# Three distances in a hand-ordered TensorE stream: mLSTM's last transposes, the softmax weights' transposes, and the last inputs of the output projections

## The chip, the cores and the metric

The kernel runs on one core of one Trainium2 chip. The metric is the device time of one execution in microseconds (us). The kernel before was run three times: 1007.92, 1008.61 and 1011.15 us, a median of 1008.61. Engines are named as in the profile: PE is TensorE (its matmuls and transposes), PEld its weight loads, DVE is VectorE, ACT is ScalarE, POOL is GpSimd, SP issues most DMAs.

## The reference

A token sequence of 256 positions with 1024 features goes through two blocks in float32. The first block has two layers. The even layer projects x to a short gated convolution (1024 wide) and to eight heads of a gated delta rule, and projects the 2048 outputs back; the odd layer does the same with 16 heads of HGRN2 (2048 outputs). Behind each come a layer norm on the residual sum and a gated addition. The second block is an attention mixer and a gated feed-forward part of width 2816. The mixer matters most here:

```python
y_fox  = _fox_attention(...)    # 6 heads, causal softmax with forget-gate bias
h_ml   = _mlstm(...)            # 4 heads
y_ml   = _from_heads(_rms(h_ml)) * ml_h_g * sigmoid(mo)
y_moba = _moba_attention(...)   # 6 heads, softmax with ALiBi bias (256 tokens: one block)
return jnp.concatenate([y_fox, y_ml, y_moba], axis=-1)
...
x = x + g1 * (y @ w_out)
```

## The kernel before, in words

Activations lie with features on partitions, in tiles of 128 features by 256 tokens. Every float32 operand of a large product is split into a high part (`hi`, `xh`, `yh`, a rounding by ACT) and a low part (`lo`, `xl`, `yl`, a subtraction by DVE), and a product of a 128 x 128 weight block is three matmuls: high by high, high weight by low input, low weight by high input. All weights of all layers lie in one stream of chunks of 16 blocks; `Stream.take` hands them out in the order in which the products use them, and splits half a chunk (8 blocks) two chunks ahead. A half can be split when the buffers of an older half are free, that is when PE has done that half's products.

PE is the only engine whose order is written by hand; the compiler's scheduler orders the others from the program's dependencies. The main line of the program issues the dense products. Beside it run generators, the side work of heads: recurrences, softmax, norms, transposes. `Side` keeps a virtual clock that advances by 0.65 with every two products (every three matmuls on 512 columns in `dense_tok`). A generator that says `yield 4.95` is taken up again when the virtual clock is 4.95 further, and its PE instructions are put into PE's stream at that place. So the number in a `yield` is a distance: how much dense work stands in PE's stream between one step of a head and the next. If the inputs of the next step aren't ready when PE comes to it, PE waits, as it works in order.

The stages follow each other as `even`, `odd`, `mixer`, `ffn`. In the mixer, `lstm` computes the four mLSTM heads in scores (`sms`), then values, divides, normalizes (DVE, with a power step on POOL, tiles `lo_`), and after its last distance transposes both token halves back (`pt`), multiplies by the gate (`y`), and splits into `yh`, `yl` as inputs 3 and 4 of the output projection. `heads` computes three groups of four query/key blocks with `dense_tok`; `head_norm` normalizes and transposes them (`sq`) into `kq` by ACT and DVE copies. `softmax_pair` does two heads: bias (transposes of `cs` and DVE), scores from `kq`, maximum, exponential and normalization into `pr`; after the distance, PE transposes the six 128 x 128 pieces of `pr` (two PSUM buffers a pair, 12 transposes for the two pairs of a group), ACT copies them (`pts`), and PE multiplies with the values. All small PSUM results of side work share four buffers (`psm`), taken in turn; a step waits until the buffer of four allocations earlier has been read. Dense results have four others (`psd`).

`out_plan` gives the order of an output projection: the first inputs over all eight output blocks, then the last `tail` = 4 inputs bank by bank (a PSUM bank holds two output blocks), so that banks finish one after the other. When a bank is finished, DVE updates x (`ready`), PE transposes x (`ln_stats`, `rms_stats`), and DVE or ACT takes the statistics. The same lists order the weight stream.

Around the change, in the program as it was:

```python
n = len(ks) - tail
return [(k, m) for k in ks[:n] for m in range(8)] + \
    [(k, m) for j in range(4) for k in ks[n:] for m in (2 * j, 2 * j + 1)]
...
OUT_PLANS = [out_plan([0, 1, 2, 3, 4, 5, 6, 8, 9, 10, 11, 7, 12, 13, 14, 15], 4),
             out_plan(list(range(16)), 4), out_plan([3, 4, 0, 1, 2, 5, 6, 7], 4)]
```

Of the kernel before, what the change touches and what calls it, by code (L numbers as in the profile page):

```python
# [60 lines left out]
def out_plan(ks, tail):  # L61


    n = len(ks) - tail
    return [(k, m) for k in ks[:n] for m in range(8)] + \
        [(k, m) for j in range(4) for k in ks[n:] for m in (2 * j, 2 * j + 1)]

# [2 lines left out]
QK_BLOCKS = [0, 1, 6, 7, 2, 3, 8, 9, 4, 5, 10, 11]  # L72

OUT_PLANS = [out_plan([0, 1, 2, 3, 4, 5, 6, 8, 9, 10, 11, 7, 12, 13, 14, 15], 4),
             out_plan(list(range(16)), 4), out_plan([3, 4, 0, 1, 2, 5, 6, 7], 4)]
DOWN_GROUPS = [[0, 1], [2, 3], [4, 5], [6], [7]]

# [122 lines left out]
class Net:  # L200
# [1020 lines left out]
    def softmax_pair(self, p_, kq, vs, yh, yl):  # L1221

        nc, ep = self.nc, self.ep
        t2 = lambda shape, tag, bufs=2: ep.tile(shape, F32, tag=tag, bufs=bufs, name=self.nm(tag))
        yield from self.wait(lambda: {(p_ // 2, 0), (p_ // 2, 1)} <= self.kqdone)
        pts = []
        for e in range(2):
            h = 2 * p_ + e
            rows = slice(64 * e, 64 * e + 64)
            q, k = kq[rows, p_], kq[rows, 6 + p_]  # L1230
            bias = t2([P, 3 * P], "bias", 3)
            if p_ < 3:
                t = self.ps("m")
                for a_ in range(2):
                    self.tr(t[:, a_ * P:(a_ + 1) * P], self.cs[:, a_, h:h + 1].to_broadcast([P, P]))
                self.tt(bias[:, :P], t[:, :P], self.c("cneg"), ALU.add)
                nc.scalar.copy(bias[:, P:2 * P], t[:, :P])
                self.tt(bias[:, 2 * P:], t[:, P:T], self.c("cneg"), ALU.add)
            else:
                nc.gpsimd.tensor_scalar(bias, self.dist, float(2.0 ** (-8.0 * (h - 5) / 6)), None, ALU.mult)  # L1240
            s = self.ps("m")
            self.mm(s[:, :P], q[:, :P], k[:, :P])
            self.mm(s[:, P:3 * P], q[:, P:], k)
            pr = t2([P, 3 * P], "pr", 6)
            mx, nm, sm = t2([P, 2], "smx"), t2([P, 2], "snm"), t2([P, 2], "ssm")
            for a_, c in ((0, slice(0, P)), (1, slice(P, 3 * P))):
                nc.vector.tensor_tensor_reduce(pr[:, c], s[:, c], bias[:, c], 1.0, -3e38, ALU.add, ALU.max, mx[:, a_:a_ + 1])
                self.ts(nm[:, a_:a_ + 1], mx[:, a_:a_ + 1], -1.0)
                self.act(pr[:, c], pr[:, c], AF.Exp, bias=nm[:, a_:a_ + 1], accum_out=sm[:, a_:a_ + 1])
            nc.vector.reciprocal(sm, sm)  # L1250
            for a_, c in ((0, slice(0, P)), (1, slice(P, 3 * P))):
                self.ts(pr[:, c], pr[:, c], sm[:, a_:a_ + 1])
            pts.append(pr)
            if e == 0:
                yield 0.65
        yield 4.95
        pt2 = []
        for e in range(2):

            pt = self.ps("m")  # L1260
            pn = t2([P, 3 * P], "pts", 6)
            for b in range(3):
                self.tr(pt[:, b * P:(b + 1) * P], pts[e][:, b * P:(b + 1) * P])
            nc.scalar.copy(pn, pt[:, :3 * P])
            pt2.append(pn)
        yield 0.65
        yield from self.wait(lambda: p_ // 2 in self.vdone or 1 in self.vdone)
        py = self.ps("m")
        for e in range(2):
            h = 2 * p_ + e  # L1270
            rows = slice(64 * e, 64 * e + 64)
            vc = 256 + 64 * h
            self.mm(py[rows, :T], vs[:, 0, vc:vc + 64], pt2[e][:, :T], stop=False)
            self.mm(py[rows, P:T], vs[:, 1, vc:vc + 64], pt2[e][:, T:], start=False)
        y = t2([P, T], "y2", 2)
        nc.scalar.copy(y, py[:, :T])
        n = p_ if p_ < 3 else p_ + 2
        self.split(yh[:, n], yl[:, n], y)
        self.ydone.add(n)
# [32 lines left out]
    def lstm(self, vs, yh, yl):  # L1312
        nc, ep = self.nc, self.ep
        t2 = lambda shape, tag, bufs=2: ep.tile(shape, F32, tag=tag, bufs=bufs, name=self.nm(tag))
        yield from self.wait(lambda: self.gated)
        va = ep.tile([P, 2, 4, 65], F32, name="va")
        nc.gpsimd.memset(va[:, :, :, 64:], 1.0)
        nc.gpsimd.tensor_copy(va[:, :, :, :64], vs[:, :, :256].rearrange("p a (h d) -> p a h d", d=64))
        sms = []
        for h in range(4):  # L1320
            rows = slice(64 * (h % 2), 64 * (h % 2) + 64)
            q, k = self.mqk[rows, h // 2], self.mqk[rows, 2 + h // 2]
            e = self.ps("m")
            for a_ in range(2):
                c = slice(2 * a_ * P, (2 * a_ + 1) * P)
                self.tr(e[:, c], self.mx[:, a_, h:h + 1].to_broadcast([P, P]))
                self.mm(e[:, c], self.bf["id"], self.bf["pos"], start=False)
            self.tr(e[:, P:2 * P], self.mx[:, 1, h:h + 1].to_broadcast([P, P]))
            et, sm = t2([P, 3 * P], "et"), t2([P, 3 * P], "smt", 4)
            self.act(et[:, :T], e[:, :T], AF.Exp, scale=-1.0, bias=self.r[:, 0, h:h + 1])  # L1330
            self.act(et[:, T:], e[:, T:3 * P], AF.Exp, scale=-1.0, bias=self.r[:, 1, h:h + 1])
            s = self.ps("m")
            self.mm(s[:, :T], k[:, :P], q)
            self.mm(s[:, T:3 * P], k[:, P:], q[:, P:])
            self.stt(sm, s[:, :3 * P], 1.0 / 32, et)
            sms.append(sm)
            yield 0.65
        os = []
        for a_ in range(2):
            pn = self.ps("m")  # L1340
            for h in range(4):
                c = slice(65 * h, 65 * h + 65)
                if a_ == 0:
                    self.mm(pn[:, c], sms[h][:, :P], va[:, 0, h])
                else:
                    self.mm(pn[:, c], sms[h][:, P:T], va[:, 0, h], stop=False)
                    self.mm(pn[:, c], sms[h][:, T:], va[:, 1, h], start=False)
            v = pn[:, :260].rearrange("p (h d) -> p h d", d=65)
            dn, ss, rs = t2([P, 4], "ldn"), t2([P, 4], "lss"), t2([P, 4], "lrs")
            self.ts(dn, v[:, :, 64], -1.0)  # L1350
            self.tt(dn, dn, v[:, :, 64], ALU.max)
            self.tt(dn, dn, self.em[:, a_], ALU.max)
            nc.vector.reciprocal(dn, dn)
            o, sq = t2([P, 4, 64], "lo_"), t2([P, 4, 64], "lsq")
            self.tt(o, v[:, :, :64], dn.unsqueeze(2).to_broadcast([P, 4, 64]))
            self.act(sq, o, AF.Square)
            nc.vector.tensor_reduce(ss, sq, AX.X, ALU.add)
            self.ts(ss, ss, 1.0 / 64, 1e-6)
            self.rsqrt(rs, ss)
            self.tt(o, o, rs.unsqueeze(2).to_broadcast([P, 4, 64]))  # L1360
            os.append(o)
            yield 0.65
        yield 4.0
        pt = self.ps("m")
        for a_ in range(2):
            for j in range(2):
                self.tr(pt[:, (2 * j + a_) * P:(2 * j + a_ + 1) * P], os[a_][:, 2 * j:2 * j + 2].rearrange("p h d -> p (h d)"))
        for j in range(2):
            y = t2([P, T], "y2", 2)
            self.stt(y, pt[:, j * T:(j + 1) * T], self.prm["ml_h_g"][:, j:j + 1], self.mo[:, j])  # L1370
            self.split(yh[:, 3 + j], yl[:, 3 + j], y)
            self.ydone.add(3 + j)
# [126 lines left out]
```

## Time and profile before

| | us |
|---|---|
| median of three runs | 1008.61 |
| the profiled execution, its time | 1007.96 |
| its span, from first to last instruction | 1006.1 |
| PE busy | 978.8 |
| DVE busy | 759.1 |
| ACT busy | 554.2 |
| POOL busy | 49.9 |

The profile is of one execution. A busy PE is not PE at its peak: the ends of matmuls are modelled and overlap with the next one's start, so the pitch of a stream is read from its starts. "Idle before" is the gap to the end of the instruction before on the same engine, and the arrow names what ended it. The granted clock is TensorE's, as a share of 2.4 GHz.

### The profile page before, as it was taken

Reading aid. Unit: us, or ns where it says so; the run is one execution under the profiler, and the core shown is the slowest. Engines: PE = TensorE matmul, PEld = TensorE weight load, DVE = VectorE, ACT = ScalarE, POOL = GpSimd, SP = SyncE. Lnnn points to the kernel's source line nnn. Section 1 sums busy time; section 2 is a strip of 40 time slices with the busy share of each in tenths; the row PEclk is TensorE's granted clock in tenths of the full one; section 3 lists DMA queues with packets and bytes.
Section 4 is the critical chain, followed back from the end, with each engine's and each line's share of the span. In section 5 each row is a group of like instructions: output and inputs, shape, how many; then the busy total and the mean of one; then the engine's idle time right before and its main releaser. Section 6 shows DMA issues by size and latency. Waiting matters only on the chain. (4 is left out here: it accounts for less than half of the span.)

```text
span 1006.1 us, 19098 instructions
## 1 busy us (share of the span) xinstructions
PE 978.8 (97%) x7622; PEld 935.6 (93%) x7622; DVE 759.1 (75%) x1459; ACT 554.2 (55%) x1098; POOL 49.9 (5%) x59
## 2 busy tenths in 40 slices
PE   6999999999999999999999999999999999999998
PEld 5999999999999999998989999997777999999998
DVE  5888876888667979889797986889577597665542
ACT  6765556644553864554545534677456674444430
POOL 1000000000000000000000000000223000000000
PEclk9999999999999999999999999999989999999999
DMA  7545523445553595655556563364323547654540
GB/s 283 191 147 177 169 86 126 166 164 177 200 195 126 185 374 208 222 201 201 210 192 230 185 215 132 111 231 135 116 84 126 189 148 272 221 199 168 185 172 22
DMA packets 34617, 179.52 MB, mean 178 GB/s; under 512 B 7648, under 2 KB 8672, under 8 KB 16608
## 3 DMA queue, kind: packets, MB, share of 16 engines
q1 hardware_dynamic: 34096, 177.71, 49.8%
q8 instruction: 60, 0.98, 0.4%
q10 hardware_dynamic: 432, 0.59, 0.2%
q14 instruction: 29, 0.24, 0.1%
HBM read 176.97 MB, written 1.31 MB: 177 GB/s over the span
## 5 line engine op out<-in xcount | busy, mean ns | idle before, releaser
L226 DVE TENSOR_TENSOR lo<-raw,hi 128x1024 fp32r<-128x1024 f32 x280 | 340.6, 1221 | 122.5 <-ACT hi L226 121.8
L226 ACT CAST hi<-raw 128x1024 fp32r<-128x1024 f32 x280 | 292.0, 1047 | 228.3 <-PE psd L312 217.6
L312 PE MATMUL psd<-xh,hi 128*128 128x256 f32 (+1 forms) x1296 | 375.6, 290 | 0.5 <-ACT hi L226 0.5
L312 PE MATMUL psd<-xl,hi 128*128 128x256 f32 (+1 forms) x1296 | 366.7, 283 | 0.4 <-DVE xl L331 0.4
L312 PE MATMUL psd<-xh,lo 128*128 128x256 f32 (+1 forms) x1296 | 366.2, 283 | 0.8 <-DVE lo L226 0.8
L312 PEld LDWEIGHTS psd<-xl,hi 128*128 128x128 f32 x1296 | 245.5, 189 | 1.4 <-DVE xl L331 1.0
L312 PEld LDWEIGHTS psd<-xh,hi 128*128 128x128 f32 x1296 | 245.0, 189 | 1.8 <-ACT hi L226 0.8
L312 PEld LDWEIGHTS psd<-xh,lo 128*128 128x128 f32 x1296 | 245.5, 189 | 1.0 <-DVE lo L226 1.0
L312 PE MATMUL psd<-yh,hi 128*128 128x256 f32 x448 | 130.6, 291 | 0.4 <-ACT yh L334 0.2
L312 PE MATMUL psd<-yl,hi 128*128 128x256 f32 x448 | 126.3, 282 | 1.2 <-DVE yl L235 1.0
L312 PE MATMUL psd<-yh,lo 128*128 128x256 f32 x448 | 126.6, 283 | 0.0
L312 PEld LDWEIGHTS psd<-yl,hi 128*128 128x128 f32 x448 | 84.8, 189 | 1.8 <-DVE yl L235 1.2
L312 PEld LDWEIGHTS psd<-yh,hi 128*128 128x128 f32 x448 | 84.7, 189 | 1.9 <-issue 0.8
L312 PEld LDWEIGHTS psd<-yh,lo 128*128 128x128 f32 x448 | 83.9, 187 | 0.0
L312 PE MATMUL psd<-hi,xh 128*128 128x512 f32 x144 | 60.9, 423 | 0.5 <-DVE lsrc L322 0.5
L1011 DVE SCALAR_TENSOR_TENSOR wa<-wa,cr 128x1024 f32<-128x1024 f32 x48 | 58.4, 1218 | 3.3 <-DMA wa<-in_w_ada_dram 2.7
L312 PE MATMUL psd<-hi,xl 128*128 128x512 f32 x144 | 57.9, 402 | 0.0
L312 PE MATMUL psd<-lo,xh 128*128 128x512 f32 x144 | 57.6, 400 | 0.0
L312 PE MATMUL psd<-al,hi 128*128 128x256 f32 x176 | 49.8, 283 | 0.0
L312 PE MATMUL psd<-ah,lo 128*128 128x256 f32 x176 | 49.7, 283 | 0.0
L312 PE MATMUL psd<-ah,hi 128*128 128x256 f32 x176 | 49.3, 280 | 0.0
L334 ACT ACTIVATE kp<-k 128x512 f32<-128x512 f32 x28 | 19.0, 679 | 33.0 <-DVE k L322 26.2
(338 smaller groups left out, 1397.8 us busy)
## 6 DMA issues: line engine op xcount, KB each, us to landing
raw<-in_w_dram SPq DMA_DIRECT2D x140, 1024.0 KB, 4.8
wa<-in_w_ada_dram SPq DMA_DIRECT2D x48, 512.0 KB, 4.5
cr<-in_c_dram SPq DMA_DIRECT2D x3, 512.0 KB, 5.7
out_dram<-fo SPq DMA_DIRECT2D x3, 256.0 KB, 2.1
cst<-in_cst_dram SPq DMA_DIRECT2D x1, 580.0 KB, 8.3
x<-in_xT_dram ACTq DMA_DIRECT2D x2, 256.0 KB, 4.0
x<-in_xT_dram SPq DMA_DIRECT2D x2, 256.0 KB, 4.8
lev<-in_lev_dram SPq DMA_DIRECT2D x1, 508.0 KB, 4.0
```

The costliest lines, as they stand in the source:

```text
L226: for i in self.nc.scalar.copy(hi, r), self.nc.vector.tensor_tensor(lo, r, hi.bitcast(F32), ALU.subtract):
L312: self.nc.tensor.matmul(out, lhsT, rhs, start=start, stop=stop, skip_group_check=True, **k)
L334: return self.nc.scalar.activation(out, a, f, bias=bias, scale=scale, **k)
L1011: self.tc.keep_in_program_order(nc.vector.scalar_tensor_tensor(w, w, 1.0, c, ALU.mult, ALU.mult, accum_out=self.md(j)[:, i % 8:i % 8 + 1]))
```

## The change

Three edits. `out_plan`: for the first two banks, the last two inputs are now used after the two before them have been used in both banks; banks 2 and 3 keep their order. The function serves all three output projections, and the weights in memory follow it. `softmax_pair`: the distance before the transposes of `pr` goes from 4.95 to 5.85. `lstm`: the distance before the last transposes goes from 4.0 to 9.75.

```diff
     n = len(ks) - tail
-    return [(k, m) for k in ks[:n] for m in range(8)] + \
-        [(k, m) for j in range(4) for k in ks[n:] for m in (2 * j, 2 * j + 1)]
+    bank = lambda ks, j: [(k, m) for k in ks for m in (2 * j, 2 * j + 1)]
+    return [(k, m) for k in ks[:n] for m in range(8)] + bank(ks[n:-2], 0) + bank(ks[n:-2], 1) + \
+        bank(ks[-2:], 0) + bank(ks[-2:], 1) + bank(ks[n:], 2) + bank(ks[n:], 3)
...
-        yield 4.95
+        yield 5.85
         pt2 = []
...
-        yield 4.0
+        yield 9.75
         pt = self.ps("m")
```

On PE, the program before has mLSTM's last transposes (`lo_`, into `psm_8684`) among the products of the second group of query and key blocks (`psd_8599`, `psd_8600`):

```order
4836 L312 MATMUL psd_8599<-hi_8480,xh_7704 128x512
4837 L312 MATMUL psd_8599<-hi_8480,xl_7705 128x512
4838 L312 MATMUL psd_8599<-lo_8481,xh_7704 128x512
4839 L315 MATMUL psm_8684<-cst,lo__1398_8591 128x128 x2
4840 L315 MATMUL psm_8684<-cst,lo__1409_8626 128x128 x2
4841 L312 MATMUL psd_8600<-hi_8480,xh_7704 128x512
```

The changed program has products there, and the transposes stand behind the last scores (`kq`) of the first softmax group:

```order
4874 L317 MATMUL psm_8808<-cst,ag_cs 128x128 x2
4875 L314 MATMUL psm_8814<-kq_8423 128x128
4876 L314 MATMUL psm_8814<-kq_8423 128x256
4877 L314 MATMUL psd_8774<-hi_8603,xh_7704 128x512
4878 L314 MATMUL psd_8774<-hi_8603,xl_7705 128x512
4879 L314 MATMUL psd_8774<-lo_8604,xh_7704 128x512
4880 L317 MATMUL psm_8849<-cst,lo__1398_8591 128x128 x2
4881 L317 MATMUL psm_8849<-cst,lo__1409_8626 128x128 x2
4882 L314 MATMUL psd_8773<-hi_8603,xh_7704 128x512
```

They moved past 18 products, eight transposes of `sq` and all scores of the group; 27 products follow before the transposes of `pr` (24 stood there in all before, now 30 from the last scores on).

On DVE, the end of the first softmax group in the program before: `sq` and `hss` are the next group's head norm, `lo` the weights' low parts, `pr` the normalizations, the second pair of which is the last:

```order
1054 L1199 TENSOR_REDUCE hss_8852<-sq_8851 128x8
1055 L1250 RECIPROCAL ssm_8810<-ssm_8810 128x2
1056 L226 TENSOR_TENSOR lo_8869<-raw_8788,hi_8868 128x1024
1057 L326 TENSOR_SCALAR pr_8807<-pr_8807,ssm_8810 128x128
1058 L326 TENSOR_SCALAR pr_8807<-pr_8807,ssm_8810 128x256
1059 L1250 RECIPROCAL ssm_8833<-ssm_8833 128x2
1060 L328 TENSOR_SCALAR hss_8852<-hss_8852 128x8
1061 L226 TENSOR_TENSOR lo_8887<-raw_8884,hi_8886 128x1024
1062 L326 TENSOR_SCALAR pr_8830<-pr_8830,ssm_8833 128x128
1063 L326 TENSOR_SCALAR pr_8830<-pr_8830,ssm_8833 128x256
1064 L322 TENSOR_TENSOR sq_8851<-psd_8600,hrs_8853 128x512
```

The same place in the changed program, where `y` and `yl` are mLSTM's outputs:

```order
1052 L328 TENSOR_SCALAR pr_8794<-pr_8794,ssm_8797 128x128
1053 L328 TENSOR_SCALAR pr_8794<-pr_8794,ssm_8797 128x256
1054 L330 TENSOR_SCALAR hss_8839<-hss_8839 128x8
1055 L333 SCALAR_TENSOR_TENSOR y_1466_8854<-psm_8849,prm,yl_1289_8005 128x256
1056 L1252 RECIPROCAL ssm_8820<-ssm_8820 128x2
1057 L324 TENSOR_TENSOR sq_8838<-psd_8600,hrs_8840 128x512
1058 L328 TENSOR_SCALAR pr_8817<-pr_8817,ssm_8820 128x128
1059 L328 TENSOR_SCALAR pr_8817<-pr_8817,ssm_8820 128x256
1060 L237 TENSOR_TENSOR yl_1287_8003<-y_1466_8854,yh_1286_8002 128x256
1061 L333 SCALAR_TENSOR_TENSOR y_1467_8858<-psm_8849,prm,yl_1289_8005 128x256
1062 L228 TENSOR_TENSOR lo_8869<-raw_8775,hi_8868 128x1024
```

The two weight subtractions moved behind the last `pr`, and the next group's `sq`, which needs POOL's `hrs`, moved ahead of it. `psm_8849` is the buffer that the fourth set of `pr` transposes takes next (`psm_8917`).

On DVE, the odd layer's output projection in the program before, where `x` is the update of a finished bank (`psd_6954` is bank 0) and BN_STATS the statistics:

```order
847 L226 TENSOR_TENSOR lo_7474<-raw_7442,hi_7473 128x1024
848 L331 SCALAR_TENSOR_TENSOR x_80<-x_80,psd_6954 128x512
849 L226 TENSOR_TENSOR lo_7512<-raw_7509,hi_7511 128x1024
850 L792 BN_STATS st_6953<-psm_7489 128x6 x2
851 L331 SCALAR_TENSOR_TENSOR x_80<-x_80,psd_6955 128x512
```

And in the changed program:

```order
847 L228 TENSOR_TENSOR lo_7473<-raw_7442,hi_7472 128x1024
848 L228 TENSOR_TENSOR lo_7512<-raw_7509,hi_7511 128x1024
849 L333 SCALAR_TENSOR_TENSOR x_80<-x_80,psd_6954 128x512
850 L333 SCALAR_TENSOR_TENSOR x_80<-x_80,psd_6955 128x512
851 L794 BN_STATS st_6953<-psm_7502 128x6 x2
```

A weight subtraction moved ahead of the update of bank 0. On PE the transposes of x for bank 0 moved 12 products (of 256 columns) later, those of the other banks not at all.

## Rows read from the trace of the kernel before

**Rows 1.** The page: span, and busy time of PE

```profile
span 1006.1 us, 19098 instructions
PE 978.8 (97%) x7622; PEld 935.6 (93%) x7622; DVE 759.1 (75%) x1459; ACT 554.2 (55%) x1098; POOL 49.9 (5%) x59
```

**Rows 2.** Waits of PE: who for whom, us in total, times, longest

```profile
PE psm L315 <- DVE lo__1398_8591 L322: 1.8, 1, 1.8
...
PE psm L315 <- DVE lo__1409_8626 L322: 1.6, 1, 1.6
...
PE psm L315 <- DVE pr L326: 1.3, 2, 1.1
PE psd L312 <- DVE yl L235: 1.0, 1, 1.0
```

**Rows 3.** Stretches around mLSTM's transposes: busy time by engine, granted clock

```profile
core 0: us, PE busy (x) PEld busy (x) DVE busy (x) ACT busy (x) POOL busy (x), PEclk, DMA share, GB/s
...
726.40:730.80 4.40, 0.97 (x6) 0.55 (x5) 2.35 (x6) 0.78 (x1) 2.46 (x2) 0.79 0.02 4
730.80:737.30 6.50, 6.50 (x20) 5.08 (x19) 3.56 (x6) 1.84 (x3) 0.00 (x0) 0.62 0.47 161
737.30:744.40 7.10, 7.10 (x39) 4.77 (x37) 4.70 (x27) 5.59 (x19) 1.64 (x1) 1.00 0.00 0
```

**Rows 4.** Timeline of PE around mLSTM's transposes: start us, us, what, idle before

```profile
726.23 0.39 PE L312 MATMUL psd<-lo,xh 128*128 128x512 f32 x1
728.47 0.41 PE L315 MATMUL psm<-cst,lo__1398_8591 128*128 128x128 f32 x2 [1.85 <-DVE lo__1398_8591 L322]
730.45 0.69 PE L315 MATMUL psm<-cst,lo__1409_8626 128*128 128x128 f32 x2 [1.58 <-DVE lo__1409_8626 L322]
730.79 0.77 PE L312 MATMUL psd<-hi,xh 128*128 128x512 f32 x1
...
737.31 1.03 PE L315 MATMUL psm<-cst,sq 128*128 128x128 f32 x8
...
739.19 0.97 PE L312 MATMUL psm<-kq 64*128 64x128 f32 x4
```

**Rows 5.** Timeline of PE: first product after the scores, first transposes of pr

```profile
744.47 0.50 PE L312 MATMUL psd<-hi,xh 128*128 128x512 f32 x1
...
750.19 1.14 PE L315 MATMUL psm<-cst,pr 128*128 128x128 f32 x9
```

**Rows 6.** Timeline of DVE: weight subtraction, copies to kq, last bias read

```profile
730.31 1.22 DVE L226 TENSOR_TENSOR lo<-raw,hi 128x1024 fp32r<-128x1024 f32 x1
...
738.60 0.29 DVE L1213 COPY kq<-psm 128x128 f32<-128x128 f32 x1 [1.71 <-ACT kq L334]
...
739.12 0.29 DVE L1213 COPY kq<-psm 128x128 f32<-128x128 f32 x1
...
745.33 0.27 DVE L322 TENSOR_TENSOR bias<-psm,cst 128x128 f32<-128x128 f32 x1
```

**Rows 7.** Timeline of POOL: the power steps of two head norms

```profile
741.13 1.64 POOL L339 TENSOR_TENSOR hrs<-hss,mhalf 128x8 f32<-128x8 f32 x1 [11.20 <-DVE hss L328]
750.32 2.48 POOL L339 TENSOR_TENSOR hrs<-hss,mhalf 128x8 f32<-128x8 f32 x1 [7.55 <-DVE hss L328]
```

**Rows 8.** Timeline of PE and DVE in the even layer's output projection

```profile
301.99 0.38 PE L312 MATMUL psd<-yh,hi 128*128 128x256 f32 x1 [0.16 <-ACT yh L234]
...
303.41 0.39 PE L312 MATMUL psd<-yl,hi 128*128 128x256 f32 x1 [1.04 <-DVE yl L235]
...
302.94 0.42 DVE L235 TENSOR_TENSOR yl<-y,yh 128x256 fp32r<-128x256 f32 x1
```

**Rows 9.** Timeline of DVE and PE in the odd layer's output projection

```profile
621.82 0.69 DVE L331 SCALAR_TENSOR_TENSOR x<-x,psd 128x512 f32<-128x512 f32 x1 [0.69 <-PE psd L312]
622.79 1.23 DVE L226 TENSOR_TENSOR lo<-raw,hi 128x1024 fp32r<-128x1024 f32 x1 [0.27 <-ACT hi L226]
...
622.94 0.28 PE L312 MATMUL psd<-yh,lo 128*128 128x256 f32 x1
623.06 0.60 PE L315 MATMUL psm<-cst,x 128*128 128x128 f32 x4
623.41 0.37 PE L312 MATMUL psd<-yh,hi 128*128 128x256 f32 x1
```

## The prediction

> **What bounds the kernel now.** I read the page's busy shares first. TensorE (PE) is busy for 978.8 of 1006.1 us [rows 1]; the reader should see that no other engine can set the end unless PE stops for it, and that all of PE's idle time together is 27.3 us. So an edit that moves PE's instructions is worth what PE waits at the places it moves, plus what TensorE's clock loses there. Second view: what PE waited for. The largest waits after the start are the two for mLSTM's tiles `lo_` (1.8 and 1.6 us); the softmax weights `pr` cost 1.3 us in two waits, and one wait of 1.0 us is for `yl`, an input of an output projection [rows 2]. These are the three things that the change moves. Third view: the stretches around the `lo_` waits. The granted clock is 0.79 in the stretch of the waits and 0.62 in the 6.5 us behind it, in which PE is always busy [rows 3]: between these waits TensorE falls from 2.4 to 1.2 GHz, and the busy stretch behind them pays for it.
>
> **mLSTM's transposes.** In the timeline [rows 4] the last product before them starts at 726.23. A product on 512 columns takes 0.238 us from start to start: 24 of them fill 744.47 to 750.19 [rows 5]. So PE is free at 726.47, but the first two transposes start at 728.47, the others at 730.45, and the next product at 730.79: 4.32 us, of which four transposes need 0.35 (what four of x take further on, 623.06 to 623.41). The 18 products behind them take 730.79 to 737.31, 6.52 us where 18 x 0.238 = 4.28 would do: 2.24 us lost to the clock. Without the transposes PE would start those 18 at 726.47, end them at 730.75, and reach the first score product (`kq`) 1.88 us later (737.31 to 739.19 in before [rows 4]), at 732.63 instead of 739.19. That is 6.56 us.
>
> What is late next: the score products need four VectorE (DVE) copies to `kq`. DVE's own chain is not moved by PE's freedom. It finishes the second `lo_` at 730.4 as before, because that waits for GpSimd, and then two weight subtractions stand ahead of the copies in the order of after: 730.31 + 2 x 1.2 = 732.7 [rows 6]. The third copy starts 0.52 later (738.60 to 739.12) and takes 0.29: 733.5. The second score product needs it. In before it was ready at 739.41, so the stage moves up by 5.9 us, not 6.56.
>
> The transposes themselves (0.35) now stand three products behind the last score product. They take the PSUM buffer that the bias transposes of four allocations earlier used, and DVE reads that last at 745.33 + 0.27 = 745.60 [rows 6], in after at 739.70. PE arrives at 744.47 - 5.9 + 3 x 0.238 = 739.28. I take a new wait of 0.4. Not seen in before, it lies between 0 (if DVE is that much earlier) and 0.9 (one more weight subtraction of 1.2 ahead of it, less the 0.3 that the copy takes). Sum for this edit: 5.9 - 0.35 - 0.4 = 5.15.
>
> Queued behind the moved steps: on DVE, `y` of head pair one stands just ahead of the last softmax normalization, and `y` of pair two behind it. The second `y` also frees the PSUM buffer that the fourth set of softmax transposes takes, so PE waits there for DVE, and DVE before that for GpSimd's power step (`hrs`). GpSimd started that step at 750.32 in before [rows 7], behind a weight subtraction of 1.2 that after puts later: 750.32 - 5.9 - 1.2 = 743.2. It takes 1.64 or 2.48 [rows 7], so it ends at 744.85 or 745.7. Behind it DVE has five passes (`sq`, two of `pr`, `yl`, `y`) that I estimate at 1.9 us together, from a copy's 0.29 and the 0.69 of a 512-column pass [rows 6, 9]: 746.75 or 747.6. PE comes at 739.70 + 0.35 + 27 x 0.238 + 1.0 (three sets of transposes) = 747.5. I put the cost at 0, with up to 0.8 for the range; the cover is the 27 products in front.
>
> Which of the two durations holds hangs on what DVE does meanwhile. In the trace 2.48 belongs to a step during which DVE subtracts weights, and 1.64 to one during which it works on PSUM. The Trainium skill (SBUF — State Buffer, section "SBUF: two separate sides") says that VectorE and GpSimd share a port pair that one of them holds for a whole instruction, a VectorE instruction with two SBUF inputs among them. By it the step takes 1.64 in after, since DVE then waits instead of subtracting; the trace agrees as far as these two rows go. By the other duration the sum would be at most 0.1 worse.
>
> **The softmax weights' transposes.** In the first two of the three groups they come six products later, 6 x 0.238 = 1.43 us. The waits there are 0.2 and 1.1 (1.3 in two, the longest 1.1 [rows 2]); both are smaller, and DVE's order is unchanged in the second group, so DVE and PE are early by the same amount. Gain 1.3; counted from start to start it could be 0.4 more, since ends of matmuls overlap. Nothing is late next: the value products behind them have the same ScalarE copies ahead of them.
>
> **The output projections.** The order of the last two inputs moves them 12 products of 256 columns later, at 0.12 us each (622.94 to 623.06 [rows 9]): 1.44 us. Even layer: PE starts one product at 301.99 and the next at 303.41 [rows 8], 1.30 us more than the pitch, because `yl` starts only at 302.94 and takes 0.42; the first of the two has 0.16 of idle ahead of it, for `yh`. Of these 1.46 the 1.44 go, with some 0.2 left if the idle counted from start to start is larger. In the mixer there is no such wait [rows 2], and the inputs keep their distance there because their transposes move by the same 12 (without that a product would come 1.44 nearer to its input); cost and gain 0. Odd layer: no wait to gain either, but the statistics of bank 0 now follow 12 products behind its completion with DVE in another order, the weight subtraction ahead of the update of x. It starts at 622.79 as before, takes 1.2, the update 0.69: 624.65, while PE's transposes of x come at 623.06 + 1.44 = 624.50 [rows 9]. New wait 0.15, between 0 and 0.7 (another update in front). In the even layer the 0.2 that may be left of the wait covers it.
>
> **Sum.** 5.15 + 1.3 + 1.44 - 0.15 = 7.74 us. The profiled execution took 1007.96 us (span 1006.1 and 1.86 around it): 1000.2. The median of the runs shown is 1008.61, so the same gain from there would be 1000.9; I predict 1000.2. From the bounds (0.4 of bank wait and 0.4 of softmax either way, the 0.65 lost to the copies) the forecast's own range is 998 to 1002.
>
> **The rivals.**
> A. The clock falls all the same. It fell between two waits, but the stretch before is thin as well (small score products of mLSTM). If that thinness is the cause, the 18 products, or as many later, still lose 2.24 us: 1002.4. Against: the granted clock is 1.00 again in 737.30 to 744.40, where PE's work is as thin [rows 3]. Chance 0.10.
> B. DVE becomes the bound of the first softmax group. If the five passes behind GpSimd are late by another weight subtraction (1.2), and the 0.8 and 0.9 above are both paid, 2.9 us of the gain come back as waits at the fourth transposes: about 1003. For: DVE has the two `y` and the two `yl` more to do in that group than before. Against: two weight subtractions that stood ahead of the last normalization now stand behind it. Chance 0.10.
> C. Slower. The many short waits that take the place of two long ones hold TensorE at 1.2 GHz through the softmax groups. There each 512-column product then costs 0.24 more; from 33 such products on, of the 96 in two groups of heads (eight inputs, two banks, three products each), the 7.7 are lost, and with 50 the time is 1012. For: the clock has fallen here once [rows 3]. Against: it did so after 3.4 us of idle in 4.3, and no new wait above exceeds 0.9. The Trainium skill names this (TensorE: Matmul & The Clock Gate, section "A second HAM failure mode: psum-queue depth-cycling"): short idle stretches between groups of matmuls can make the clock fall again and again. By that rule C would hold; the row for 737.30 to 744.40, groups with short pauses at 1.00, does not agree. Chance 0.03.
> D. The moves don't do what they say: both `lo_` waits return one for one at the score products, since DVE and GpSimd set the pace of the whole stage, and the 5.15 are gone: 1005.4. Against: DVE was idle for about half of 726.4 to 730.8 (busy 2.35 of 4.40 [rows 3]). Chance 0.04.
>
> **How the numbers follow.** The forecast has 0.73. A difference of 0.3% (3 us) is what a measurement can tell here. Forecast, A and B are faster, D is on the border and mostly the same: faster 0.94, same 0.03, slower 0.03. The range is 997.5 to 1003.5: it takes in the unknown costs, A and most of B.
>
> **What would show it.** Right: no PE wait for `lo_` above 0.5; granted clock 1.00 from 726 to the end of the softmax groups; the first score product about 6 us earlier; no wait for `pr` above 0.3; the wait for `yl` at most 0.2; a short new wait of PE on DVE at the mLSTM transposes' PSUM buffer and at the odd layer's transposes of x. Wrong: a stretch at half clock anywhere but the two ends, a PE wait above 1 us at the fourth softmax transposes, or later stages (the feed-forward part) that lose what these gained.

## The result, and the profile after

The changed kernel takes 998.99 us (median of 4 runs, 998.32 to 999.79), the kernel before beside it 1008.26 (1007.28 to 1011.15): ratio 0.9904, 95% interval 0.9882 to 0.9926. That is faster by clearly more than 0.3%. The forecast was 1000.2, its range 997.5 to 1003.5. The profiled execution took 999.43 us with a span of 997.6, so that span against span the gain is 8.5 us where the sum said 7.74. The page after, which answers to [rows 1]:

```profile
span 997.6 us, 19099 instructions
...
PE 976.0 (98%) x7622; PEld 934.0 (94%) x7622; DVE 758.3 (76%) x1459; ACT 553.4 (55%) x1098; POOL 49.1 (5%) x59
...
PEclk9999999999999999999999999999999999999999
```

PE's idle time went from 27.3 to 21.6 us, its busy time by 2.8: the first is the waits, the second mostly clock (the number of matmuls is the same). In the list of PE's waits the rows of [rows 2] are all missing, and two short ones are new (the first row is the start, as before). Columns as there:

```profile
PE psm L314 <- ACT xh L236: 4.8, 1, 4.8
...
PE psm L314 <- DVE kq L1215: 0.3, 1, 0.3
PE psm L317 <- DVE bias L324: 0.2, 1, 0.2
```

The stretches that answer to [rows 3], with PE's granted clock:

```profile
725.10:729.40 4.30, 4.30 (x21) 3.42 (x20) 2.25 (x6) 1.86 (x2) 2.49 (x2) 1.00 0.00 0
729.40:736.00 6.60, 6.27 (x34) 4.22 (x33) 5.94 (x25) 4.74 (x15) 1.64 (x1) 1.00 0.45 159
736.00:745.00 9.00, 8.78 (x40) 6.57 (x40) 7.05 (x34) 5.35 (x17) 2.78 (x2) 1.00 0.00 0
```

The first is the stretch in which PE used to wait: it is busy for all of it, at 2.4 GHz, as in the other two. In PE's timeline [rows 4, 5] the products now run up to the head norm's transposes, and mLSTM's own stand behind the scores:

```profile
729.13 0.39 PE L314 MATMUL psd<-lo,xh 128*128 128x512 f32 x1
729.37 1.03 PE L317 MATMUL psm<-cst,sq 128*128 128x128 f32 x8
...
730.94 0.38 PE L317 MATMUL psm<-cst,ag_cs 128*128 128x128 f32 x2
731.65 1.09 PE L314 MATMUL psm<-kq 64*128 64x128 f32 x4 [0.33 <-DVE kq L1215]
...
737.62 0.40 PE L314 MATMUL psd<-lo,xh 128*128 128x512 f32 x1
738.24 0.44 PE L317 MATMUL psm<-cst,lo__1398_8591 128*128 128x128 f32 x2 [0.22 <-DVE bias L324]
738.52 0.38 PE L317 MATMUL psm<-cst,lo__1409_8626 128*128 128x128 f32 x2
738.65 0.48 PE L314 MATMUL psd<-hi,xh 128*128 128x512 f32 x1
...
745.05 1.47 PE L317 MATMUL psm<-cst,pr 128*128 128x128 f32 x12
```

All twelve `pr` transposes run in one piece: before it was nine, a wait, and three.

To compare kernels I cut each trace at four points on PE: the first `rs` transposes of the even and of the odd layer, the first mLSTM product `va,smt`, and the last `mrs` transposes, behind the softmax groups. Each entry is the difference of two start times (us), for the profiled execution; the last column is the clock's fall to 1.2 GHz inside the fourth stretch.

| kernel | start to even `rs` | to odd `rs` | to `va` | `va` to `mrs` | to the end | fall |
|---|---|---|---|---|---|---|
| before | 319.31 | 316.93 | 81.24 | 101.07 | 187.59 | 6.83 |
| changed | 317.67 | 317.15 | 81.39 | 93.83 | 187.57 | none |
| e1, mLSTM alone | 320.78 | 316.94 | 81.34 | 96.21 | 187.58 | none |
| e2, softmax alone | 320.02 | 316.98 | 81.37 | 99.06 | 187.59 | 6.83 |
| e3, projections alone | 319.53 | 317.16 | 81.68 | 100.14 | 187.58 | 3.41 |
| e4, new order in the even layer only | 318.87 | 316.92 | 81.49 | 93.82 | 187.56 | none |
| e5, mLSTM half way | 320.03 | 316.98 | 81.39 | 98.86 | 187.57 | 3.41 |
| e5, mLSTM ahead of the scores | 319.73 | 316.99 | 81.86 | 100.71 | 187.57 | 10.24 |
| e6, even only, 10.4 | 317.73 | 316.97 | 81.38 | 93.41 | 187.58 | none |

Changed less before, by columns: -1.64, +0.22, +0.15, -7.24, -0.02. The gain lies where it was forecast. The first column varies by two us between executions of one kernel (below). The third varies by some tenths, but in e9, the changed kernel again (below), it was 83.09: ScalarE waited 3.90 us there for the transfer of a small weight (`ag_raw`), 2.13 in the changed kernel's first profile, and everything behind came later.

```profile
674.44 0.30 ACT L236 CAST nwh<-ag_raw 128x128 fp32r<-128x128 f32 x1 [3.90 <-DMA ag_raw<-in_w_sm_dram]
```

The last column varies too: e3 has the same `lo_` waits as before (1.8 and 1.6 us) and a fall half as long, and one of its eleven runs had a granted clock of 1.000.

The even layer's gain is clearer in a shorter stretch. From the 300th matmul ahead of the first even `rs` transposes, which lies inside the output projection, to these transposes it is 37.37 to 37.51 us in the five profiles with the old order there (before, e1, e2 and both e5) and 35.93 to 36.10 in the seven with the new order, 1.47 less in the mean.

### The profile page after: what moved, and what is told of

It is laid out like the page before. It is cut to its first block, busy times and chain, and to the rows that moved or that the text cites. A ratio compares the mean times of both kernels' runs of the same rounds, so it can differ in the third digit from the quotient of the medians.

```text
span 997.6 us, 19099 instructions
## 1 busy us (share of the span) xinstructions
PE 976.0 (98%) x7622; PEld 934.0 (94%) x7622; DVE 758.3 (76%) x1459; ACT 553.4 (55%) x1098; POOL 49.1 (5%) x59
## 4 chain that ended last, share of the span: by engine, by line
PE 82%; DVE 10%; DMA 3%; ACT 3%; issue 2%; POOL 0%; SPq 0%; POOLq 0%; DVEq 0%; ACTq 0%
PE psd L314 68%; PE psm L314 11%; DVE lo L228 3%; PE psm L317 3%; DMA raw<-in_w_dram 1%; ACT hi L228 1%; DVE q L324 1%; DVE xl L333 1%; DVE at L942 1%; DMA ti<-dti 1%; DMA wa<-in_w_ada_dram 1%; DVE wa L1013 0%; DVE mt L333 0%; DMA ag_raw<-in_w_sm_dram 0%; DVE k L324 0%
```

## The experiments

**Each edit alone.** e1 is the kernel before with the mLSTM distance alone, e2 with the softmax distance alone, e3 with the new `out_plan` alone:

```
e1:  -        yield 4.0      +        yield 9.75     (mLSTM)
e2:  -        yield 4.95     +        yield 5.85     (softmax)
e3:  out_plan as in the change, both distances as before
```

> mLSTM's longer distance alone (9.75), the rest as before. My theory (PE waits for lo_, and the clock falls because of these waits): both lo_ waits go, the granted clock stays 1.00 around 726 to 737, the first score product comes 5.9 us earlier, and about 5 us are gained, less a wait of up to 0.8 us at the fourth set of softmax transposes, which come six products nearer to the second y on VectorE than in the full change; the wait of 1.1 us for pr in the second group stays. Time 4.5 to 5.9 us under the kernel before. Rival (thin work sets the clock, not the waits): the clock falls near 729 all the same, 2.2 us less gained, 2.5 to 3.5 us under. Rival (VectorE and GpSimd pace the stage): under 1.5 us gained.

> The softmax weights' longer distance alone (5.85), the rest as before. My theory: the two waits for pr (0.2 and 1.1 us idle, 1.7 us by starts) go, nothing else moves; the lo_ waits (3.4 us) and the fall of the clock stay: 1.3 to 1.7 us under the kernel before. Rival (the wait comes back at the value products or at the output projection's last two inputs, which now have twelve products less ahead of them): 0 to 0.5 us under, with a PE wait for pts, y or yl in the mixer.

> The new order of the output projections alone, the rest as before. My theory: the even layer's wait of 1.5 us for yh and yl goes, the odd layer gets a wait of 0.15 to 0.25 us at the transposes of x, the mixer changes nothing: 1.2 to 1.5 us under the kernel before; the lo_ waits and the fall of the clock stay. Rival (the layer norm behind, which waits for the last bank, takes the gain back): 0 to 0.3 us under, with a longer wait for rs before the even layer's gate.

Measured: e1 1004.97 us, ratio 0.9958 (0.9943 to 0.9973); e2 1006.81, 0.9977 (0.9966 to 0.9989); e3 1008.11, 0.9992 (0.9978 to 1.0006), which time alone doesn't tell from nothing. By medians e1 gains 4.0 us, less than the 4.5 to 5.9 expected, e2 2.15, more than the 1.3 to 1.7, and e3 0.85, less than the 1.2 to 1.5; five of e1's seven runs had a granted clock of 0.998, and where it fell in them is not recorded. In the fourth stretch e1 gains 4.86 and e2 2.01, together 6.87 of the full change's 7.24. In e1's profile the `lo_` waits and the fall of the clock are gone, and what is missing shows in PE's timeline at the fourth set of `pr` transposes, the place that rival B named:

```profile
746.52 1.15 PE L315 MATMUL psm<-cst,pr 128*128 128x128 f32 x9
748.44 0.52 PE L315 MATMUL psm<-cst,pr 128*128 128x128 f32 x3 [0.78 <-DVE y L331]
```

and on DVE, which runs up to that `y` behind GpSimd:

```profile
746.24 0.69 DVE L322 TENSOR_TENSOR sq<-psd,hrs 128x512 f32<-128x512 f32 x1 [1.36 <-POOL hrs L339]
746.85 0.72 DVE L326 TENSOR_SCALAR pr<-pr,ssm 128x128 f32<-128x128 f32 x2
747.49 0.41 DVE L235 TENSOR_TENSOR yl<-y,yh 128x256 fp32r<-128x256 f32 x1
747.82 0.47 DVE L331 SCALAR_TENSOR_TENSOR y<-psm,prm,yl 128x256 f32<-128x256 f32 x1
```

Of the 5.25 us that e1 is ahead at the first `pr` transposes, 4.86 are left at the end of the stretch. So about 0.4 us of the mLSTM edit need the softmax edit: its six products more in front of the `pr` transposes hide DVE's chain up to the second `y`. In e2 both `pr` waits are gone, while the `lo_` waits and the fall stay as in [rows 2, 3]. In e3 the wait for `yl` is gone and the second stretch is 0.23 longer. Its fourth stretch is 0.93 shorter than before though the `lo_` and `pr` waits are all there: the clock's fall was shorter in this execution, so about a us of e1's 4.86 hangs on which execution of before it is held against.

**The new order in the even layer only.** e4 is the changed kernel, with the old order kept for the odd layer and the mixer:

```
-OUT_PLANS = [out_plan([0, 1, ... 15], 4), ...
+OUT_PLANS = [late_plan([0, 1, ... 15], 4), ...   (late_plan: the new order; out_plan: the old)
```

> Both longer distances, but the new order in the even layer's projection alone; the odd layer's and the mixer's keep the old order. My theory: the odd layer's new wait at the transposes of x goes (0.2 us better than the full change), and the mixer's old order costs nothing, since the wait list of before has none there and about four microseconds of products stand between: 0.1 to 0.3 us under the full change, 9.4 us under the kernel before. Rival (the mixer needs its late order, as its softmax transposes come twelve products later): a PE wait for yh or yl at the last two inputs of the mixer's projection, 0.5 to 1.5 us over the full change.

Measured 1001.02 us, ratio 0.9918 (0.9901 to 0.9935). The second stretch is back at 316.92 and the last is unchanged: the new order costs 0.22 us in the odd layer and is worth nothing in the mixer. Its total is nevertheless above the changed kernel's, where 0.1 to 0.3 us under it was expected. In its profile the clock fell to 1.2 GHz in the startup, for which the edits are no reason (next but one), and all four of its runs had a granted clock of 0.998.

**What the clock's fall hangs on.** Two kernels with the mLSTM distance in between, everything else as before:

```
e5_lstm_half:   -        yield 4.0      +        yield 5.3
e5_lstm_ahead:  -        yield 4.0      +        yield 7.9
```

> The kernel before with one number changed: the distance in front of mLSTM's last transposes is 5.3 instead of 4.0, so that they stand six products of 512 columns later (1.43 us of work), still in front of the other twelve and of the scores. Before, PE waited 1.85 and 1.58 us there and its clock then fell for 6.8 us. Both theories expect waits of about 0.4 and 1.6 us. Theory one, the clock falls for the two waits together, and with 2.0 us instead of 3.4 it stays up: the way from the odd layer's layer norm to the mixer's shortens by the 1.4 of the waits and the 2.2 of the clock, 3.6 us, and the time goes to about 1005. Theory two, the clock falls for the thin work of the stage or for the second wait alone: the granted clock falls again right behind the transposes, only the 1.4 is gained, and the time is about 1007.

> The kernel before with one number changed: the distance in front of mLSTM's last transposes is 7.9, so that they stand behind all eighteen products that follow them in the kernel before, but in front of the transposes and products of the scores. The lo_ waits are gone as with 9.75. On DVE the two y and the two yl (0.87 and 0.82 us in the kernel before) then stand behind both weight subtractions and directly in front of the four copies to kq. Theory one, the gain of the mLSTM edit is limited by what DVE has in front of those copies: the first score product moves up by 4.2 us only (the 5.9 of the prediction less 1.7), PE waits about 2 us for kq, the mixer is reached about 4.2 us earlier, and none of it is lost to the PSUM buffers afterwards (no wait on bias, none on y in front of the fourth set of pr transposes). Theory two, the gain is PE's own wait and clock and DVE has room: 6.2 us at the first score product and a wait for kq below 0.5.

The half way kernel: 1006.32 us, ratio 0.9971 (0.9957 to 0.9985), and 2.21 us less in the fourth stretch, between both theories (3.6 and 1.4). PE's timeline has waits of 0.45 and 1.58, and then the pitch of the products goes from 0.23 to 0.43:

```profile
729.39 0.41 PE L315 MATMUL psm<-cst,lo__1398_8591 128*128 128x128 f32 x2 [0.45 <-DVE lo__1398_8591 L322]
731.38 0.44 PE L315 MATMUL psm<-cst,lo__1409_8626 128*128 128x128 f32 x2 [1.58 <-DVE lo__1409_8626 L322]
...
732.12 0.39 PE L312 MATMUL psd<-lo,xh 128*128 128x512 f32 x1
732.35 0.39 PE L312 MATMUL psd<-hi,xh 128*128 128x512 f32 x1
...
735.09 0.63 PE L312 MATMUL psd<-hi,xl 128*128 128x512 f32 x1
735.52 0.63 PE L312 MATMUL psd<-lo,xh 128*128 128x512 f32 x1
```

The fall is half as long as in the kernel before (3.41 us), and not every execution has one: four of ten ran at a granted clock of 1.000, at 1004.1 to 1005.5 us, which is theory one's figure; the others at 0.997 or 0.998 (where in the program they lost it, the mean doesn't say). So the waits that are left bring a fall in the profiled execution and none in these four, and neither theory holds for all.

The kernel with the transposes ahead of the scores: 1008.68 us, ratio 0.9987 (0.9970 to 1.0005), no gain that can be told. Both theories missed the total. The first had the way to the scores nearly right (4.58 us against 4.2, a wait of 1.58 against about 2), but not that it would be lost behind them. PE's timeline, and the granted clock of the stretches:

```profile
731.50 0.39 PE L312 MATMUL psd<-lo,xh 128*128 128x512 f32 x1
731.73 0.38 PE L315 MATMUL psm<-cst,lo__1398_8591 128*128 128x128 f32 x2
...
735.71 1.14 PE L312 MATMUL psm<-kq 64*128 64x128 f32 x4 [1.58 <-DVE kq L1213]
...
744.67 0.63 PE L312 MATMUL psd<-hi,xl 128*128 128x512 f32 x1
```

```profile
732.60:737.60 5.00, 3.42 (x20) 2.33 (x19) 4.92 (x17) 3.77 (x10) 0.00 (x0) 1.00 0.62 210
737.60:747.80 10.20, 10.20 (x27) 6.43 (x26) 5.56 (x34) 3.18 (x15) 1.64 (x1) 0.50 0.00 0
```

The `lo_` waits are gone, and the first score product comes 17.13 us after the first `va` product, against 21.71 before and 15.44 in e1 and the changed kernel. The 1.69 between the last two is what DVE does in front of the copies to `kq`, two `y` and two `yl` (0.87 + 0.82): DVE's queue does limit the stage, as the prediction had it. But PE's one wait of 1.58 now stands in front of the scores, whose products are small, and behind it the clock falls for 10.24 us. That the fall is so long because the products are small is not shown. The stage's gain of 4.58 is gone by the `mrs` transposes (100.71 against 101.07). Its two runs at a clock of 1.000 took 1004.15 and 1004.75, the nine at 0.992 to 0.995 1007.0 to 1011.4.

**The startup, and the even layer's new order with a longer mLSTM distance.** e6 has e4's order and puts mLSTM's transposes three products further back; e7 is the changed kernel again, beside it. e8 and e9 are the same two once more.

```
e6, e8:  -        yield 9.75     +        yield 10.4    (and late_plan in the even layer only)
```

> The changed kernel once more, beside e6 on the same chip. Theory one, the fall of the clock in the first 25 us that e3 and e4 showed (3.4 us long, 1.5 us lost) comes by run, not by kernel: some execution of this kernel or of e6 shows it too, or the profiles show it here and not there without any edit to the startup. Theory two, it belongs to the kernels with part of the change: the changed kernel has 999.0 us and a granted clock of 1.000 throughout again. By both the stages from the even layer's norm to the mixer's take the same time as in its first profile, within 0.2 us.

> The changed kernel with the new order of the output projection in the even layer alone, and mLSTM's last transposes three products (0.71 us) further back. Theory: the short wait of the transposes for the PSUM buffer that DVE's bias read frees (0.39 us by starts in the changed kernel) goes, and so does the odd layer's 0.2: 0.6 us less than the changed kernel, 998.4. Rival: the two y on DVE now come later too, the fourth set of pr transposes waits for the second y as in e1 (0.8 to 1.0 there), and the time is the changed kernel's or up to 0.5 more.

> The kernel of e6 once more (new output order in the even layer alone, mLSTM's last transposes three products further back). Its runs before were of two kinds: three at a granted clock of 1.000 near 998.6 us and three at 0.998 near 1001.7. Theory: the kinds come by run, from the fall of the clock in the first 25 us; among runs at 1.000 this kernel is 0.6 to 1.3 us under the changed kernel (998.4 to 998.9 against 999.7 to 1000.7 so far), and the stage between the odd layer's norm and the mixer takes 174.8 us again. Rival: the lower time was that session's, and the runs at 1.000 of both kernels overlap.

> The changed kernel, beside e8 on the same chip. Theory: runs at a granted clock of 1.000 between 999.0 and 1000.5 us, a few at 0.998 about 2 us above, and the stage between the odd layer's norm and the mixer 175.2 to 175.6 us. Rival: no difference from e8.

Measured: e7 1000.09 us, 0.9914 (0.9896 to 0.9932); e6 999.96, 0.9914 (0.9892 to 0.9937); e9 1000.27, 0.9914 (0.9897 to 0.9931); e8 1000.48, 0.9918 (0.9901 to 0.9934). The wait for `bias` is not in the lists of e6 and e8. No wait for `y` is listed in its place, but by starts there is one of 0.06 (0.39 from the third to the fourth set of `pr` transposes, 0.33 in the changed kernel): the rival, in small. The fourth stretch is 93.41 and 93.45 against 93.83, 93.83 and 93.81 in the three profiles of the changed kernel, the second 316.97 and 316.92 against 317.15 to 317.19. These 0.6 us are what the theory expected. The times can't show them: at a clock of 1.000 e6 ran at 998.4 to 998.9 and e8, the same program, at 1000.2 to 1000.5, on both sides of the changed kernel. So e8's theory for the times failed, and its rival came true.

Two more expectations were missed. In e7 the way from the even layer's norm to the mixer's took 0.38 more than in the first profile, where 0.2 was the bound. In e9 the stage between the odd layer's norm and the mixer's took 176.90, where 175.2 to 175.6 was expected, because of the transfer above.

The startup's fall is settled by the changed kernel itself. e7 first, then e9, in the same stretches:

```profile
18.00:21.20 3.20, 1.51 (x14) 1.36 (x14) 3.18 (x9) 3.17 (x5) 0.00 (x0) 1.00 0.26 46
21.20:24.60 3.40, 3.40 (x34) 3.22 (x31) 3.05 (x13) 3.40 (x6) 0.00 (x0) 1.00 0.70 282
```

```profile
18.00:21.20 3.20, 1.50 (x14) 1.41 (x14) 3.09 (x9) 3.17 (x5) 0.00 (x0) 1.00 0.28 44
21.20:24.60 3.40, 3.40 (x19) 3.08 (x18) 2.20 (x8) 2.57 (x5) 0.00 (x0) 0.50 0.66 272
```

In both PE waits 1.7 us for `gm` and is busy 1.5 of 3.2 us; behind that one execution keeps 2.4 GHz and the other has 3.4 us at 1.2 GHz. e9's first products with `T` come 122.72 us after its start, e7's 121.20 (121.20 to 122.35 in the eight profiles without this fall, 122.72 to 123.43 in the four with it: e3, e4, e5 ahead of the scores and e9). So e4's total (and e3's first column) says nothing against the even-only order, and the stretches decide.

## Why the prediction was right

**mLSTM's transposes** (forecast 5.15). Right in mechanism; that the size fits so well is in part luck, as two errors cancel. From the first `va` product to the first `pr` transposes e1 is 5.25 us shorter than before (27.46 against 32.71), the changed kernel 5.30 (28.84, less the 1.43 of the six products now in front). Term by term: the stage moved up by 6.27 (first score product 15.44 after `va`, was 21.71), not 5.9. The wait for `kq` is 0.33, where 5.9 implied 0.66 of loss against PE's own 6.56: DVE was quicker through its queue than I set it. The first copy starts 2.27 behind the start of the two subtractions (I took 2.4), and the third copy 0.40 behind the first (0.52 in [rows 6], where copies waited for ScalarE):

```profile
729.04 2.35 DVE L228 TENSOR_TENSOR lo<-raw,hi 128x1024 fp32r<-128x1024 f32 x2
731.31 0.28 DVE L1215 COPY kq<-psm 128x128 f32<-128x128 f32 x1
731.51 0.28 DVE L1216 COPY kq<-psm 128x128 f32<-128x128 f32 x1
731.71 0.28 DVE L1215 COPY kq<-psm 128x128 f32<-128x128 f32 x1
```

The transposes cost 0.41 (0.35), the new wait for the buffer 0.39 by starts (0.4). Two small losses weren't in the forecast: from the first score product to the next dense product behind the scores it is 5.41 us (5.28 before), and the first product behind mLSTM's transposes takes 0.09 more than the pitch. So 6.27 - 0.41 - 0.39 - 0.22 = 5.25: the stage came 0.37 earlier than forecast and lost 0.27 more behind. The clock's part, 2.24, came back whole, as the 18 products stand in a stretch at 1.00; measured against an execution like e3's, with half the fall, it would have been less.

**The softmax weights** (forecast 1.3). Right in sign, too small. e2's fourth stretch is 2.01 shorter. I took idle time as the profile shows it (1.3) and only allowed for the 1.7 by start times, which was the better measure. From the first of the twelve transposes to the product behind them, the second group took 2.68 us before and 1.28 in e2, before first:

```profile
769.74 1.14 PE L315 MATMUL psm<-cst,pr 128*128 128x128 f32 x9
771.96 0.70 PE L315 MATMUL psm<-cst,pr 128*128 128x128 f32 x3 [1.08 <-DVE pr L326]
772.42 0.48 PE L312 MATMUL psd<-hi,xh 128*128 128x512 f32 x1
```

```profile
771.39 1.52 PE L315 MATMUL psm<-cst,pr 128*128 128x128 f32 x12
772.67 0.48 PE L312 MATMUL psd<-hi,xh 128*128 128x512 f32 x1
```

The first group took 1.82 and 1.23. That is 1.40 and 0.59, nearly all of the 2.01. It is more than the late start of the last three transposes, because behind the wait they also stand further apart: 0.46 from the first of them to the next product, 0.30 and 0.25 in e2. This term makes up 0.6 to 0.7 of the 0.8 by which the sum is too low.

**The output projections** (forecast +1.44, -0.15 and 0). Right. The even layer gains 1.47 by the shorter stretch above. What is left of the wait is 0.19 over the pitch of 0.12, as forecast:

```profile
302.92 0.28 PE L314 MATMUL psd<-yh,hi 128*128 128x256 f32 x1
303.23 0.39 PE L314 MATMUL psd<-yl,hi 128*128 128x256 f32 x1
```

The odd layer loses 0.22 (the forecast's own terms, 622.79 + 1.2 + 0.69, make a wait of 0.18 and not 0.15); there the update of x for bank 0 stands behind the subtraction as [rows 9] suggested, and PE's transposes of x follow it, 0.17 late against the pitch of 0.12:

```profile
621.13 1.23 DVE L228 TENSOR_TENSOR lo<-raw,hi 128x1024 fp32r<-128x1024 f32 x1 [1.65 <-ACT hi L228]
622.27 1.45 DVE L333 SCALAR_TENSOR_TENSOR x<-x,psd 128x512 f32<-128x512 f32 x2
...
622.72 0.28 PE L314 MATMUL psd<-yh,lo 128*128 128x256 f32 x1
623.01 0.66 PE L317 MATMUL psm<-cst,x 128*128 128x128 f32 x4
```

The mixer gives 0 (e4's last column against the changed kernel's).

**The rivals.** A: wrong for the change (1.00 throughout), but e5 half way shows that a fall can stay where waits of 0.45 and 1.58 stay. B: its mechanism is real and sits where it was put, at the second `y`; in the changed kernel the cover of 27 products holds, in e1 with 21 it doesn't. The spare time is about 0.4 us: the fourth set starts 0.59 behind the end of the second `y`, against 0.15 in e1, where PE waited for it. C, the slower side, did not come true, but e5 ahead of the scores is its case in small: one wait of 1.58 in front of small products and 10.24 us at 1.2 GHz. Two readings in C were wrong. Its row for 737.30 to 744.40 has PE busy for 7.10 of 7.10 us, so it shows no pauses that left the clock at 1.00; and a product on 512 columns costs 0.20 more at 1.2 GHz (0.43 against 0.23), not 0.24. The Trainium skill (TensorE: Matmul & The Clock Gate, section "A second HAM failure mode: psum-queue depth-cycling") speaks of short idle stretches between groups of matmuls; here the two waits of 0.33 and 0.22 in the changed kernel left the clock at 1.00, so the trace doesn't bear the rule out at that length. D fell: the waits didn't come back.

GpSimd's power step ahead of the last normalization took the shorter of the two durations of [rows 7], as chosen, while DVE waited for it:

```profile
741.72 1.64 POOL L341 TENSOR_TENSOR hrs<-hss,mhalf 128x8 f32<-128x8 f32 x1 [6.36 <-DVE hss L330]
```

```profile
743.39 0.69 DVE L324 TENSOR_TENSOR sq<-psd,hrs 128x512 f32<-128x512 f32 x1 [1.36 <-POOL hrs L341]
```

That agrees with the port pair of the Trainium skill (SBUF — State Buffer, section "SBUF: two separate sides"); no run here tries the other case on purpose.

By medians the gain is 9.3 us and not 8.5: the profiled execution of before was 0.3 us under its median, that of the changed kernel 0.4 over its. In the three later comparisons the 55 runs of before had granted clocks of 0.993 to 0.998, while 12 of 15 runs of the changed kernel had 0.999 or 1.000.

## What to carry to other kernels

A wait of PE costs its own length and, in many executions, time at half clock behind it. The longest fall here stood behind a wait in front of small products; that what PE does next sets its length is a guess from these profiles. Moving the waiting step behind dense work paid here; look at where the wait goes if the producer is late all the same. A longer distance on one chain moves its later passes on the shared engines too (here `y` on DVE, which frees a PSUM buffer of the softmax), so two distances may have to grow together. Count waits by start times against the usual pitch, not by the idle time that the profile prints.

## What the runs showed of the hardware

TensorE's clock does not fall in every execution with the same waits: in the startup it did in e9 and not in e7, one program, for 1.5 us of time; and of e5 half way four executions of ten ran at a full 1.000, though its profile has a fall of 3.4 us. With the same two `lo_` waits the fall lasted 6.83 us in before and e2 and 3.41 in e3, and one run of e3 was at 1.000; what decides it stays open. The falls in the profiles lasted 3.41, 6.83 or 10.24 us, and in them a product of 512 columns took 0.43 us instead of 0.23. A profile without a fall in one stretch therefore doesn't prove that the program is free of it; the list of granted clocks over many runs does more.
